# One stationary operand for the high and low gate weights of an mLSTM, and a first weight word in two transfers

## The chip, the cores and the metric

The kernel runs on one core of a Trainium2 chip. Five engines with instruction queues of their own take part: TensorE (PE, matmuls), VectorE (DVE), ScalarE (ACT), GpSimd (POOL) and SyncE (SP, which here only issues transfers). The metric is the device time of one execution in microseconds (us), as a median over runs.

## The reference

A trunk of two layers over 256 tokens of width 1024; the feed-forward width is 2816. All of it is computed in float32.

```
for l in range(2):
    x = layer_norm(ALPHA * x + 0.5 * swiglu(x, ffn_w_in[l, 0], ffn_w_out[l, 0]), ...)
    y = mlstm_mixer(x, ...) if l == 0 else window_attention(x, ...)
    x = layer_norm(ALPHA * x + y, ...)
    x = layer_norm(ALPHA * x + 0.5 * swiglu(x, ffn_w_in[l, 1], ffn_w_out[l, 1]), ...)

# swiglu: (silu(x @ w_gate) * (x @ w_up)) @ w_out
# mlstm_mixer, 4 heads, both directions:
p = x @ w_in                      # q, k, v, o, and 16 columns of gates
gates = p[..., 3072:] + gate_b    # input and forget gate, for each direction and head
logf = log_sigmoid(f_pre); g = cumsum(logf)
# weights exp(g_t - g_s + ig_s - m_t) between tokens, where m is a running maximum
# h = (weights * (q @ k)) @ v / max(|sum|, exp(-m)); both directions are added
# window_attention: 16 query heads, 4 key heads, |t - s| <= 128, a slope on the distance,
# a sink for each head in the softmax's denominator
```

## The kernel before

**High and low parts.** PE's fast float format (fp32r) keeps fewer bits than float32. So every operand is split in two: `hi`, the value rounded to fp32r, and `lo`, what is left. A product of two float32 matrices becomes three matmuls into the same accumulator, `hi*hi`, `hi*lo` and `lo*hi` (`mm3`). A weight word is a block of 128 x 1024 values (512 KB): SP brings it to a tile `raw`, ACT casts it to `w_hi`, DVE subtracts to get `w_lo` (`word`, `split`). The activations are kept transposed as `xT_hi` and `xT_lo`: PE turns a 128x128 block against the identity (`ident`), ACT or DVE casts the result, DVE subtracts. In the feed-forward parts sums of blocks (`S1` to `S4`, and `b` among the weights) let seven block products do the work of eight (`seven`).

**Order.** The kernel's functions don't issue instructions; they record them in a `Book`, from which all are emitted at the end. That is why every row of the profile bears one line, L472. PE's order is the order of the code. `cost` gives each step a planned duration, `latest` works back from PE's line to a due time of each step, and `sequence` lets each of DVE, ACT, POOL and SP take the step with the earliest due time among those that are ready in the plan. So a changed figure in `cost` moves all due times ahead of it, and with them the order on four engines.

**Start.** SP's first transfers are half of the first 128 tokens of x (256 KB), the first weight word (512 KB), half of the other tokens, and the next word. PE turns the identity 8 times, then x's first four blocks, then the identity 14 times more (`warm(14)`), whose results are not used. The first word is cast in two halves on ACT and DVE, each of which waits for the whole transfer. Then come the first products, `pw<-w_hi,xT_hi`.

**Gates.** The 16 gate columns lie in two tiles of 128 x 8 x 128 with zeros between them, `gw_hi` and `gw_lo`: input gates in output rows 0 to 63, forget gates in rows 64 to 127, the two directions 32 rows apart. For each of 8 blocks of the width `mm3` multiplies them with `xT`, 24 matmuls of 256 columns in all, into `pg`. DVE and ACT make the logarithm of the sigmoid and the sums and maxima along the tokens from it (tiles `scan` and `ig`), and PE turns the result later (`pw<-ident,ig`).

**Attention.** At its setup POOL builds the table of distances (`fwd`, `back`, `dist`) and takes a step of the layer norm (`rs`). Then for each of 8 pairs of heads: PE makes scores (`pw<-kT,q`); DVE adds slope and distance and takes the maximum (`ISA` in the order of instructions, CUSTOM_DVE in the profile, to `sc` and `nse`); ACT takes the exponential and sums it (`ACTIVATE sc,nse`); DVE adds the sink's part and takes the reciprocal (`nse`); POOL scales `sc` by it; PE turns the four tiles (`pw<-ident,sc`); ACT and DVE split the result (`pr0`, `pr1`); PE multiplies with the values (`pw<-pr,v`). PE fills the time between with products for later heads and of the output (`py<-w_hi,q_hi`).

Of the kernel before, what the change touches and what calls it, by code (L numbers as in the profile page):

```python
# [170 lines left out]
class Book:  # L171


    def __init__(self, nc, pools):
        self.nc, self.pools = nc, pools
        self.steps, self.rooms = [], {kind: [] for kind in HOMES}
        self.tensor, self.vector, self.scalar = Queue(self, "PE"), Queue(self, "DVE"), Queue(self, "ACT")
        self.gpsimd, self.sync = Queue(self, "POOL"), Queue(self, "SP")
        self.loaded, self.table_users = None, []

# [67 lines left out]
    def cost(self, s):  # L248
# [3 lines left out]
        if s.engine == "PE":  # L252
            n = size(s.outs[0])
            s.takes, s.later = (109.0 if s.name == "transpose" else n / 2.4 + 13.3), 200.0
            if s.name == "matmul" and s.args[1].shape[0] == 64:
                s.takes = 111.0
        elif s.name == "dma_start":
# [218 lines left out]
def trunk_kernel(ctx: ExitStack, tc: tile.TileContext, x, ffn_w_in, ffn_w_out, ln_g, ln_b, ml_w_in, ml_gate_b,  # L476
# [21 lines left out]
    def pair(p, *idx):  # L498
        return p[0][idx], p[1][idx]
# [36 lines left out]
    def two(w, r0, c0):  # L536
        return w[r0:r0 + 256, c0:c0 + 512].rearrange("(k p) f -> p k f", p=128)

    def wide(w, r0, c0, **kw):
        return split(word(two(w, r0, c0), 2), **kw)  # L540

# [169 lines left out]
    def ffn(l, i, n, pending, last):  # L711
# [28 lines left out]
        if start:  # L740
            gu(0)
            load_x(1, 0)
            warm(14)

# [227 lines left out]
    def mlstm(l, n, pending, last):  # L972
        va = [both(f"v{t}", (128, 4, 272), "tall") for t in range(2)]
        gwi = both("gw", (128, 8, 128))
        for p in gwi:
            nc.gpsimd.memset(p.bitcast(F32), 0.0)
        for g in range(4):
            c = 64 * (g % 2) + 32 * (g // 2)
            split_evac(pair(gwi, A, A, slice(c, c + 4)), gw[:, :, 4 * g:4 * g + 4])
        for t in range(2):  # L980
# [34 lines left out]
        nc.vector.tensor_scalar(fa, fe, 1.0, None, op0=OP.add)  # L1015
        nc.vector.scalar_tensor_tensor(fa, fa, 1.0, fe, op0=OP.subtract, op1=OP.subtract)
        nc.vector.tensor_sub(fl, fa, fl)
        nc.vector.tensor_add(fm, fm, fl)
        cum = fl
        u = ig  # L1020
        for d in range(2):
            q = slice(32 * d, 32 * d + 32)
            ord_ = slice(None, None, -1) if d else A
            nc.vector.tensor_tensor_scan(cum[q, ord_], ones[q].to_broadcast([32, S]), fm[q, ord_], 0.0, op0=OP.mult, op1=OP.add)
        nc.vector.tensor_sub(u, ig, cum)
        pm = fm
        for d in range(2):
# [3 lines left out]
        for d in range(2):  # L1031
            nc.gpsimd.dma_start(most[0:128:32, d], pm[32 * d:32 * d + 4])
        ex = fe
        nc.vector.scalar_tensor_tensor(ex, cum, -1.0, pm, op0=OP.mult, op1=OP.subtract)
# [19 lines left out]
        def weights(h):  # L1054
# [3 lines left out]
            for d, blk in ((0, 1), (1, 0)):  # L1058
                c = 32 * d + h
# [53 lines left out]
        def divide(h):  # L1113
            den, ys = part.pop(h)
            nc.vector.tensor_max(den, den, ecol[:, :, h:64:32])
            nc.vector.reciprocal(den, den)
# [294 lines left out]
```

## Time and profile before

| | |
|---|---|
| median of 3 runs | 913.88 us (913.88 to 913.98) |
| the profiled execution | 913.72 us, its span 911.8 us |
| mean granted clock of PE | 0.997 |
| PE busy | 902.6 us, 4459 matmuls |
| DVE busy | 811.4 us |
| ACT busy | 584.2 us |
| POOL busy | 145.4 us |
| moved by transfers | 208.53 MB |

The span is the time between the first and the last instruction of the profiled execution; what lies around it (1.9 us) belongs to the execution's time. A row of the timeline gives the start in us from the span's start, the busy time of the row's instructions in us, the engine, the line, the operation with its tiles (written tile, arrow, read tiles), the sizes and the number of instructions that the row joins; in brackets the idle time of the engine before it, and what it waited for. Matmuls overlap in their pipeline: the busy time of a row is longer than the step from one matmul to the next.

### The profile page before, as it was taken

The page shows a single profiled execution, that of the slowest core. Times are in us where ns is not written, and L with a number is a line of the kernel's source. Part 1 is how long each engine was busy: PE and PEld are TensorE (multiplying, and loading weights), DVE is VectorE, ACT ScalarE, POOL GpSimd, SP SyncE. Part 2 cuts the span into 40 slices and gives each one's busy share as a digit, 9 for nine tenths or more (in the row PEclk, how much of TensorE's full clock was granted, in tenths as well). Part 3 has the DMA queues.
Part 4 walks back from the last instruction along what each step waited for, and adds up shares of the span by engine and source line. Part 5 has one row for each costly group of instructions (what it writes and reads, how often), then busy time and mean ns, then how long its engine had stood idle before and what let it go on. Part 6 is the DMA issues. An engine that isn't in the chain of part 4 may idle for free.

```text
span 911.8 us, 12602 instructions
## 1 busy us (share of the span) xinstructions
PE 902.6 (99%) x4459; PEld 757.3 (83%) x4459; DVE 811.4 (89%) x985; ACT 584.2 (64%) x793; POOL 145.4 (16%) x177
## 2 busy tenths in 40 slices
PE   9999999999999999999999999999999999999996
PEld 7888888889988888888888888888898888888885
DVE  7989999887798989999889899998998698999976
ACT  7676777548554667776646667775488555677760
POOL 0112111206011011111011121211513202111100
PEclk9999999999999999999999999999999999999998
DMA  9999998844494688988965989989452367999831
GB/s 329 388 311 218 299 307 231 282 151 142 137 309 149 198 200 252 289 262 241 364 224 167 240 204 317 278 240 336 142 162 94 131 213 152 260 282 236 293 70 47
DMA packets 100703, 208.53 MB, mean 229 GB/s; under 512 B 6904, under 2 KB 21264, under 8 KB 100640
## 3 DMA queue, kind: packets, MB, share of 16 engines
q1 hardware_dynamic: 82944, 174.09, 54.6%
q0 software_dynamic: 17696, 33.65, 21.4%
q8 instruction: 35, 0.57, 0.3%
q14 instruction: 28, 0.23, 0.1%
HBM read 206.65 MB, written 1.05 MB: 228 GB/s over the span
## 4 chain that ended last, share of the span: by engine, by line
PE 93%; DVE 3%; ACT 1%; issue 1%; POOL 0%; DMA 0%; DVEq 0%; POOLq 0%
PE pw L472 60%; PE py L472 33%; DVE w_lo L472 1%; DVE x L472 1%; ACT sc L472 1%; DVE pr L472 0%; DMA x<-in_x_dram 0%; DVE stats L472 0%; ACT pr L472 0%; ACT w_hi L472 0%; POOL sc L472 0%; DVE xT_lo L472 0%; DVE sc L472 0%; DVE few L472 0%; POOL rs L472 0%
## 5 line engine op out<-in xcount | busy, mean ns | idle before, releaser
L472 ACT CAST w_hi<-b 128x1024 fp32r<-128x1024 f32 x224 | 234.1, 1055 | 88.8 <-PE py L472 44.1
L472 DVE TENSOR_TENSOR w_lo<-b,w_hi 128x1024 fp32r<-128x1024 f32 x224 | 267.0, 1218 | 17.5 <-ACT w_hi L472 17.1
L472 ACT CAST w_hi<-raw 128x1024 fp32r<-128x1024 f32 (+1 forms) x181 | 186.8, 1047 | 97.9 <-PE py L472 63.5
L472 DVE TENSOR_TENSOR w_lo<-raw,w_hi 128x1024 fp32r<-128x1024 f32 (+1 forms) x181 | 218.2, 1224 | 21.3 <-ACT w_hi L472 19.7
L472 PE MATMUL pw<-w_hi,xT_hi 128*128 128x512 f32 x480 | 189.5, 396 | 0.0
L472 PE MATMUL pw<-w_hi,xT_lo 128*128 128x512 f32 x480 | 187.1, 391 | 0.1
L472 PE MATMUL pw<-w_lo,xT_hi 128*128 128x512 f32 x480 | 186.2, 390 | 0.0
L472 PE MATMUL pw<-w_hi,S 128*128 128x512 f32 x512 | 162.8, 389 | 0.0
L472 POOL DMA_DIRECT2D b<-in_ffn_w_in_dram x64 | 77.4, 1211 | 470.3 <-DVE b L472 272.5
L472 PE MATMUL py<-w_hi,h_hi 128*128 128x512 f32 x317 | 125.2, 395 | 0.0
L472 PE MATMUL py<-w_hi,h_lo 128*128 128x512 f32 x317 | 123.6, 390 | 0.0
L472 PE MATMUL py<-w_lo,h_hi 128*128 128x512 f32 x317 | 123.5, 389 | 0.0
L472 PEld LDWEIGHTS pw<-w_hi,S 128*128 128x128 f32 x512 | 96.1, 188 | 19.9
L472 PEld LDWEIGHTS pw<-w_hi,xT_lo 128*128 128x128 f32 x480 | 90.0, 188 | 20.2 <-DVE xT_lo L472 0.9
L472 PEld LDWEIGHTS pw<-w_lo,xT_hi 128*128 128x128 f32 x480 | 90.3, 188 | 17.8
L472 PEld LDWEIGHTS pw<-w_hi,xT_hi 128*128 128x128 f32 x480 | 90.0, 188 | 17.4 <-ACT xT_hi L472 0.2
L472 PE MATMUL pw<-w_lo,S 128*128 128x512 f32 x256 | 99.6, 389 | 0.0
L472 DVE TENSOR_TENSOR b<-b,b 128x1024 f32<-128x1024 f32 x64 | 78.1, 1221 | 1.2
L472 PEld LDWEIGHTS py<-w_hi,h_lo 128*128 128x128 f32 x317 | 59.5, 188 | 12.6
L472 PEld LDWEIGHTS py<-w_lo,h_hi 128*128 128x128 f32 x317 | 59.6, 188 | 11.9
L472 PEld LDWEIGHTS py<-w_hi,h_hi 128*128 128x128 f32 x317 | 59.6, 188 | 11.7
L472 PEld LDWEIGHTS pw<-w_lo,S 128*128 128x128 f32 x256 | 48.0, 188 | 10.0
(198 smaller groups left out, 1079.0 us busy)
## 6 DMA issues: line engine op xcount, KB each, us to landing
b<-in_ffn_w_in_dram SPq DMA_DIRECT2D x128, 512.0 KB, 7.0
raw<-in_ffn_w_out_dram SPq DMA_DIRECT2D x88, 512.0 KB, 7.4
b<-in_ffn_w_in_dram POOLq DMA_DIRECT2D x64, 512.0 KB, 8.6
raw<-in_ffn_w_in_dram SPq DMA_DIRECT2D x32, 512.0 KB, 7.3
raw<-in_ml_w_in_dram SPq DMA_DIRECT2D x24, 512.0 KB, 9.2
raw<-in_ffn_w_in_dram SPq DMA_DIRECT2D x32, 256.0 KB, 6.6
raw<-in_at_w_in_dram SPq DMA_DIRECT2D x12, 512.0 KB, 8.5
raw<-in_ml_w_out_dram SPq DMA_DIRECT2D x8, 512.0 KB, 4.6
```

Of the source, the lines that this page charges most:

```text
L472: getattr(engines[s.engine], s.name)(*[real(x) for x in s.args], **{k: real(x) for k, x in s.kw.items()})
```

## The change

Three edits, and the new orders that follow from the third.

1. The gates' high parts stand in columns 0 to 63 and their low parts in columns 64 to 127 of one stationary tile `gwi`. For each of the 8 blocks it is multiplied with `xT_hi` and `xT_lo`: 16 matmuls. The products with the low part come out in rows 64 to 127 of `pg`; ACT copies these rows to `gl`, and the additions that bring in the bias on DVE add `gl` too. (`lo*lo`, which was left out before, is now part of the sum.) Both directions share the forget gate's steps of 32 rows. One memset on POOL goes.
2. The first word comes in two transfers of 128 x 512 values (`halves`), each with its own cast and subtraction, and `warm(14)` becomes `warm(4)`.
3. `cost` plans a matmul with 64 rows of contraction with 58.5 ns for 111, and adds 88 ns wherever PE goes from such matmuls to others or back.

```
         if s.engine == "PE":
             n = size(s.outs[0])
             s.takes, s.later = (109.0 if s.name == "transpose" else n / 2.4 + 13.3), 200.0
-            if s.name == "matmul" and s.args[1].shape[0] == 64:
-                s.takes = 111.0
+            narrow = s.name == "matmul" and s.args[1].shape[0] == 64
+            if narrow:
+                s.takes = 58.5
+            if narrow != self.narrow:
+                s.takes, self.narrow = s.takes + 88.0, narrow
...
-    def wide(w, r0, c0, **kw):
-        return split(word(two(w, r0, c0), 2), **kw)
+    def wide(w, r0, c0, halves=False):
+        src = two(w, r0, c0)
+        return split(word([src[:, k:k + 1] for k in range(2)] if halves else src, 2), halves=halves)
...
-            r = 64 * (g % 2) + 32 * (g // 2)
+            r = 32 * (g % 2) + 4 * (g // 2)
             nc.gpsimd.dma_start(gbias[r:r + 4], ml_gate_b[0, 4 * g:4 * g + 4].rearrange("(p o) -> p o", o=1))
...
-            warm(14)
+            warm(4)
...
-        gwi = both("gw", (128, 8, 128))
-        for p in gwi:
-            nc.gpsimd.memset(p.bitcast(F32), 0.0)
+        gwi = nc.tile("gw", (128, 8, 128), "big", FR)
+        nc.gpsimd.memset(gwi.bitcast(F32), 0.0)
         for g in range(4):
-            c = 64 * (g % 2) + 32 * (g // 2)
-            split_evac(pair(gwi, A, A, slice(c, c + 4)), gw[:, :, 4 * g:4 * g + 4])
+            c = 32 * (g % 2) + 4 * (g // 2)
+            split_evac((gwi[:, :, c:c + 4], gwi[:, :, 64 + c:68 + c]), gw[:, :, 4 * g:4 * g + 4])
...
         for k in range(8):
-            mm3(pg, pair(gwi, A, k), pair(xT, A, k), k == 0, k == 7)
+            for f in range(2):
+                nc.tensor.matmul(pg, gwi[:, k], xT[f][:, k], start=k == f == 0, stop=k == 7 and f == 1)
         scan = nc.tile("scan", (128, 4, S), "big")
         fa, fe, fl, fm = [scan[0:64, n_] for n_ in range(4)]
-        ig = temp("ig", S)[0:64]
-        nc.vector.tensor_scalar(fa, pg[64:128], gbias[64:128], None, op0=OP.add)
-        nc.vector.tensor_scalar(fm, pg[64:128], gbias[64:128], 0.0, op0=OP.add, op1=OP.min)
-        nc.vector.tensor_scalar(ig, pg[0:64], gbias[0:64], None, op0=OP.add)
-        nc.vector.scalar_tensor_tensor(fa, fm, 2.0, fa, op0=OP.mult, op1=OP.subtract)
-        nc.scalar.activation(fe, fa, AF.Exp)
-        nc.scalar.activation(fl, fe, AF.Ln, bias=1.0)
+        gl, ig = temp("gl", S)[0:64], temp("ig", S)[0:64]
+        nc.scalar.copy(gl, pg[64:128])
+        r, f_ = slice(0, 32), slice(32, 64)
+        nc.vector.scalar_tensor_tensor(fa[r], pg[f_], gbias[f_], gl[f_], op0=OP.add, op1=OP.add)
+        nc.vector.tensor_scalar(fm[r], fa[r], 0.0, None, op0=OP.min)
+        nc.vector.scalar_tensor_tensor(fa[r], fm[r], 2.0, fa[r], op0=OP.mult, op1=OP.subtract)
+        nc.scalar.activation(fe[r], fa[r], AF.Exp)
+        nc.scalar.activation(fl[r], fe[r], AF.Ln, bias=1.0)
+        for d in range(2):
+            nc.vector.scalar_tensor_tensor(ig[32 * d:32 * d + 32], pg[r], gbias[r], gl[r], op0=OP.add, op1=OP.add)
...
```

The lines left out keep the steps of the scans, with 32 rows where both directions share them and 36 in place of 32 between the directions' results.

The orders: ACT at the start of the program, before. Names end in the number of the buffer; `raw_79`, `raw_91` and `raw_98` are the first three words, `py` the turned blocks of x, `S3` a sum of two of them.

```order
L472 CAST w_hi_118<-raw_79 128x512 x2
L472 CAST xT_hi_71<-py_133 128x4x128
L472 CAST w_hi_145<-raw_91 128x1024
L472 COPY x10_153<-py_133 128x512
L472 CAST xT_hi_71<-py_161 128x4x128
L472 CAST w_hi_176<-raw_98 128x1024
L472 CAST xT_hi_71<-py_166 128x4x128
L472 CAST S3_190<-S3_169 128x512
L472 CAST w_hi_197<-raw_108 128x1024
```

The same place now; the first three words are `raw_79`, `raw_93` and `raw_106`.

```order
L475 CAST w_hi_109<-raw_79 128x512 x2
L475 CAST xT_hi_71<-py_123 128x4x128
L475 COPY x10_134<-py_123 128x512
L475 CAST w_hi_142<-raw_93 128x1024
L475 CAST S3_150<-S3_145 128x512
L475 CAST xT_hi_71<-py_154 128x4x128
L475 CAST xT_hi_71<-py_161 128x4x128
L475 CAST w_hi_174<-raw_106 128x1024
L475 CAST S1_183<-S1_169 128x512
```

The third word's cast now stands behind the cast of S3 and both casts of x; it stood ahead of S3 and of the second of them.

DVE in attention, heads 0 and 1, before: `nse_6262` belongs to head 0, `sc_6318` and `nse_6319` to head 1, each a pair of heads.

```order
L472 ISA nse_6262 128x1
L472 TENSOR_TENSOR nse_6262<-nse_6262 128x4
L472 RECIPROCAL nse_6262<-nse_6262 128x4
L472 SCALAR_TENSOR_TENSOR q1_lo_6244<-py_6234,qs_col_6051,q1_hi_6238 128x256
L472 ISA sc_6318,nse_6319<-pw_6288,dist_6027,few_74 128x256
L472 ISA nse_6319 128x1
```

The same place now, where `nse_6246` belongs to head 0, `sc_6292` and `nse_6293` to head 1.

```order
L475 ISA nse_6246 128x1
L475 ISA sc_6292,nse_6293<-pw_6272,dist_5993,few_74 128x256
L475 ISA nse_6293 128x1
L475 TENSOR_TENSOR nse_6246<-nse_6246 128x4
L475 RECIPROCAL nse_6246<-nse_6246 128x4
```

The first score step of head 1 moved ahead of head 0's sum and reciprocal, for which POOL's scaling waits. The same happens between heads 1 and 2 and between heads 4 and 5.

ACT at the end of attention, before: `pr0_6795` and `pr1_6809` are head 5's, `sc_6815`, `sc_6830` and `nse_6816` head 7's, `pr0_6859` and `pr1_6864` head 6's.

```order
L472 CAST pr0_6795<-pw_6767 128x512
L472 CAST pr1_6809<-pw_6797 128x512
L472 ACTIVATE sc_6815,nse_6816<-sc_6815,nse_6816 128x256
L472 ACTIVATE sc_6830,nse_6816<-sc_6830,nse_6816 128x256
L472 ACTIVATE sc_6815,nse_6816<-sc_6815,nse_6816 128x256
L472 ACTIVATE sc_6830,nse_6816<-sc_6830,nse_6816 128x256
L472 ACTIVATE nse_6816<-nse_6816,few_74 128x2
L472 CAST pr0_6859<-pw_6849 128x512
L472 CAST pr1_6864<-pw_6854 128x512
L472 ACTIVATE nse_6816<-nse_6816,few_74 128x2
L472 CAST q1_hi_6238<-pw_6822 128x256
L472 ACT_TABLE_LOAD
```

The same place now, where `pr0_6778` and `pr1_6820` are head 5's, `pr0_6850` and `pr1_6858` head 6's.

```order
L475 CAST pr0_6778<-pw_6754 128x512
L475 ACTIVATE sc_6787,nse_6788<-sc_6787,nse_6788 128x256
L475 ACTIVATE sc_6803,nse_6788<-sc_6803,nse_6788 128x256
L475 ACTIVATE sc_6787,nse_6788<-sc_6787,nse_6788 128x256
L475 CAST pr1_6820<-pw_6785 128x512
L475 ACTIVATE sc_6803,nse_6788<-sc_6803,nse_6788 128x256
L475 ACTIVATE nse_6788<-nse_6788,few_74 128x2 x2
L475 ACT_TABLE_LOAD
L475 CAST q1_hi_6222<-pw_6811 128x256
L475 CAST pr0_6850<-pw_6840 128x512
L475 CAST pr1_6858<-pw_6847 128x512
```

Head 5's second cast moved behind three of head 7's exponentials, and head 7's sums and the table load moved ahead of head 6's casts. On POOL at attention's setup two of the selects for `fwd` and `back` moved ahead of the step on `rs`; PE's order is the same as before but for the gates and the ten turns.

More of the change, by code (lines that the diff above doesn't have):

```diff
@@ L178, in __init__ @@
         self.gpsimd, self.sync = Queue(self, "POOL"), Queue(self, "SP")
-        self.loaded, self.table_users = None, []
+        self.loaded, self.table_users, self.narrow = None, [], False
     def tile(self, name, shape, kind, dtype=F32):
@@ L1004, in mlstm @@
         for k in range(8):
-            mm3(pg, pair(gwi, A, k), pair(xT, A, k), k == 0, k == 7)
+            for f in range(2):
+                nc.tensor.matmul(pg, gwi[:, k], xT[f][:, k], start=k == f == 0, stop=k == 7 and f == 1)
         scan = nc.tile("scan", (128, 4, S), "big")
         fa, fe, fl, fm = [scan[0:64, n_] for n_ in range(4)]
-        ig = temp("ig", S)[0:64]
-        nc.vector.tensor_scalar(fa, pg[64:128], gbias[64:128], None, op0=OP.add)
-        nc.vector.tensor_scalar(fm, pg[64:128], gbias[64:128], 0.0, op0=OP.add, op1=OP.min)
-        nc.vector.tensor_scalar(ig, pg[0:64], gbias[0:64], None, op0=OP.add)
-        nc.vector.scalar_tensor_tensor(fa, fm, 2.0, fa, op0=OP.mult, op1=OP.subtract)
-        nc.scalar.activation(fe, fa, AF.Exp)
-        nc.scalar.activation(fl, fe, AF.Ln, bias=1.0)
[L1015 to L1019, printed above, removed]
+        gl, ig = temp("gl", S)[0:64], temp("ig", S)[0:64]
[8 more added lines that the diff above has]
+            nc.vector.scalar_tensor_tensor(ig[32 * d:32 * d + 32], pg[r], gbias[r], gl[r], op0=OP.add, op1=OP.add)
+        nc.vector.tensor_scalar(fa[r], fe[r], 1.0, None, op0=OP.add)
+        nc.vector.scalar_tensor_tensor(fa[r], fa[r], 1.0, fe[r], op0=OP.subtract, op1=OP.subtract)
+        nc.vector.tensor_sub(fl[r], fa[r], fl[r])
+        nc.vector.tensor_add(fm[r], fm[r], fl[r])
+        cum = fe
         u = ig
@@ L1023, in mlstm @@
             ord_ = slice(None, None, -1) if d else A
-            nc.vector.tensor_tensor_scan(cum[q, ord_], ones[q].to_broadcast([32, S]), fm[q, ord_], 0.0, op0=OP.mult, op1=OP.add)
+            nc.vector.tensor_tensor_scan(cum[q, ord_], ones[r].to_broadcast([32, S]), fm[r, ord_], 0.0, op0=OP.mult, op1=OP.add)
         nc.vector.tensor_sub(u, ig, cum)
-        pm = fm
+        pm = fl
         for d in range(2):
@@ L1031, in mlstm @@
         for d in range(2):
-            nc.gpsimd.dma_start(most[0:128:32, d], pm[32 * d:32 * d + 4])
-        ex = fe
+            nc.gpsimd.dma_start(most[0:128:32, d], pm[36 * d:36 * d + 4])
+        ex = cum
         nc.vector.scalar_tensor_tensor(ex, cum, -1.0, pm, op0=OP.mult, op1=OP.subtract)
@@ L1058, in weights @@
             for d, blk in ((0, 1), (1, 0)):
-                c = 32 * d + h
+                c = 36 * d + h
                 nc.scalar.activation(w[:, d, 2], w[:, d, blk], AF.Exp, bias=ucol[:, 1 - blk, c:c + 1], scale=-1.0)
@@ L1114, in divide @@
             den, ys = part.pop(h)
-            nc.vector.tensor_max(den, den, ecol[:, :, h:64:32])
+            nc.vector.tensor_max(den, den, ecol[:, :, h:64:36])
             nc.vector.reciprocal(den, den)
```

## The prediction

> **What bounds the kernel now.** I read the busy line first, then the chain of work that ended last, then the waits of PE alone.
>
> ```profile
> PE 902.6 (99%) x4459; PEld 757.3 (83%) x4459; DVE 811.4 (89%) x985; ACT 584.2 (64%) x793; POOL 145.4 (16%) x177
> PE 93%; DVE 3%; ACT 1%; issue 1%; POOL 0%; DMA 0%; DVEq 0%; POOLq 0%
> ```
> ```profile
> PE py L472 <- DVE ident L472: 1.7, 1, 1.7
> ```
> PE is busy for 902.6 of 911.8 us, it makes 93% of the chain, and the list of its waits holds one entry, the wait for the identity at the start. So an edit counts for what it takes from PE's instructions or from the short gaps between them, and DVE at 89% is the engine that can open new gaps. The list leaves short gaps out; they are read below from the starts of successive matmuls.
>
> **The start (first word in two transfers, 4 turns for 14).** The timeline of the first 14 us, PE, then ACT, then DVE: start, busy time, engine, operation, and in brackets the idle time before it with what ended it.
>
> ```profile
> 1.71 1.97 PE L472 MATMUL py<-ident 128*128 128x128 f32 x8 [1.71 <-DVE ident L472]
> 3.77 1.11 PE L472 MATMUL py<-ident,x 128*128 128x128 f32 x4
> 4.67 2.31 PE L472 MATMUL py<-ident 128*128 128x128 f32 x14
> 6.74 0.71 PE L472 MATMUL pw<-w_hi,xT_hi 128*128 128x512 f32 x2
> 7.29 0.60 PE L472 MATMUL py<-ident,x 128*128 128x128 f32 x4
> 13.89 0.39 PE L472 MATMUL pw<-w_lo,xT_hi 128*128 128x512 f32 x1
> ```
> ```profile
> 5.74 0.91 PE L472 MATMUL py<-ident 128*128 128x128 f32 x6
> ```
> ```profile
> 5.58 1.14 ACT L472 CAST w_hi<-raw 128x512 fp32r<-128x512 f32 x2 [3.50 <-DMA raw<-in_ffn_w_in_dram]
> 10.69 0.59 ACT L472 CAST xT_hi<-py 128x512 fp32r<-128x512 f32 x1 [0.59 <-PE py L472]
> 11.23 1.05 ACT L472 CAST w_hi<-raw 128x1024 fp32r<-128x1024 f32 x1
> ```
> ```profile
> 4.92 0.69 DVE L472 CAST xT_hi<-py 128x512 fp32r<-128x512 f32 x1 [3.26 <-PE py L472]
> 6.25 1.28 DVE L472 TENSOR_TENSOR w_lo<-raw,w_hi 128x512 fp32r<-128x512 f32 x2
> 12.32 1.23 DVE L472 TENSOR_TENSOR w_lo<-raw,w_hi 128x1024 fp32r<-128x1024 f32 x1 [0.25 <-ACT w_hi L472]
> ```
> The ten turns that go ran from 4.67 to 6.98, while ACT waited for the word and cast it (5.58 + 1.14 = 6.72). They filled waiting, so taking them out gains nothing by itself; what can gain is the word. The first x (256 KB) was there at 3.77 and the word (512 KB) at 5.58, so I put its first half at their middle, 4.7 (an estimate), and its cast at 0.57 (half of 1.14) later. The first product then waits for the high part of x on DVE, 4.92 + 0.69 = 5.61, and starts at about 5.7 instead of 6.74; the second waits for the second half, which lands no earlier than the whole did: 5.58 + 0.57 = 6.15. Behind them stand four turns of the second x, the next transfer in SP's queue. At the word's rate (0.9 per 256 KB) it lands at 6.5; the split puts one more issue ahead of it, for which no row has a price, so I take 6.9, which is 0.4 before the 7.29 of now.
>
> That lead doesn't last. On ACT the third word's high half now stands behind the sum S3 and both casts of x. The last four of the second pair of turns would end near 10.7, the cast of x behind them (0.59) at 11.4, the word's high half (1.05) at 12.45 and its low half on DVE (1.23) at 13.7. Before, the low half was ready at 12.32 + 1.23 = 13.55 for a product at 13.89, so a product 0.35 earlier (13.54) has to wait for it until about 13.8. I take -0.1, nearest to what this chain allows. The bounds are -0.45 (the lead stays whole, when ACT gets through sooner) and +0.2 (the third word 0.3 later still).
>
> At the start the chip's clock matters too: four turns took 1.11 us at 3.77 and 0.60 at 7.29, and the six from 5.74 (0.91) hold one last wide step, so the pace doubled near 5.9, when PE had run nothing but turns, 4.2 us after the first. I count the switch at the same time after the change, since its 16 turns start at the same moments. The Trainium skill, "TensorE: Matmul & The Clock Gate", Part 4: PE-mode transpose, has it that transposes don't count as busy work and that with them the full rate "doesn't engage"; then the switch would come only with the products. These rows disagree, for the pace doubled before any product ran; by the row the term is 0, by the rule it is the rival B below.
>
> **The gates.** The timeline of PE, DVE and ACT there:
>
> ```profile
> 194.88 0.28 PE L472 MATMUL pw<-xT_hi,gw_hi 128*128 128x256 f32 x1
> ...
> 197.63 0.28 PE L472 MATMUL pw<-xT_hi,gw_lo 128*128 128x256 f32 x1
> ```
> ```profile
> 197.96 0.89 DVE L472 TENSOR_SCALAR scan<-pw,few 64x256 f32<-64x256 f32 x2 [1.57 <-PE pw L472]
> ...
> 204.87 0.42 DVE L472 SCALAR_TENSOR_TENSOR scan<-scan 64x256 f32<-64x256 f32 x1
> ```
> ```profile
> 199.39 0.87 ACT L472 ACTIVATE scan<-scan 64x256 f32<-64x256 f32 x2 [3.72 <-DVE scan L472]
> ```
> ```profile
> 208.75 0.34 PE L472 MATMUL pw<-ident,ig 64*128 64x64 f32 x2
> ```
> The first of the 24 matmuls starts at 194.88, the last at 197.63: 2.75 / 23 = 0.1196 each. Eight go: -0.96, all on PE, which is the bound there. Nothing was idle for the operands before them, so I take it whole; its bounds are -0.96 and 0 (if the chain behind becomes late). That chain of scans ends at 204.87 + 0.42 = 205.29 and PE turns its result at 208.75, a cover of 3.46. Added to it are a copy of 64 rows on ACT (at most 0.44, an Exp of the same size being half of 0.87), one more addition on DVE (at most 0.45, half of 0.89), one word's cast now ahead of the Exp on ACT (1.05) and one word's subtraction inside the chain on DVE (1.23): 3.17 in all, still under 3.46. The end of the gates' matmuls comes 0.96 earlier, and so do the turns, so the two move together. The missing memset on POOL frees POOL, which has no part in the path here. If the cover went, PE would wait at 208.75 by what exceeds it.
>
> **Setup of attention.** Only the planner's order changes here: POOL does two of its selects for the distance table in the 5.43 us in which it had waited for `rs`.
>
> ```profile
> 644.75 1.53 POOL L472 TENSOR_TENSOR rs<-rs,few 128x1 f32<-128x1 f32 x1 [5.43 <-DVE rs L472]
> ...
> 650.67 2.13 POOL L472 TENSOR_TENSOR dist<-fwd,back 128x512 f32<-128x512 f32 x1
> ```
> ```profile
> 645.78 1.22 DVE L472 TENSOR_TENSOR w_lo<-raw,w_hi 128x1024 fp32r<-128x1024 f32 x1
> ...
> 651.92 1.97 DVE L472 TENSOR_TENSOR w_lo<-raw,w_hi 128x1024 fp32r<-128x1024 f32 x1
> 653.81 1.27 DVE L472 TENSOR_TENSOR xT_lo<-py,xT_hi 128x512 fp32r<-128x512 f32 x2
> ```
> ```profile
> 653.82 0.39 PE L472 MATMUL pw<-w_hi,xT_hi 128*128 128x512 f32 x1
> 654.05 0.39 PE L472 MATMUL pw<-w_lo,xT_hi 128*128 128x512 f32 x1
> 654.54 0.50 PE L472 MATMUL pw<-w_hi,xT_lo 128*128 128x512 f32 x1
> 654.88 0.40 PE L472 MATMUL pw<-w_hi,xT_hi 128*128 128x512 f32 x1
> ```
> The steps of 0.49 and 0.34 between these products, against the 0.23 of the first step, are 0.38 of waiting for the low part of x. DVE came to it late because its subtraction took 1.97 beside POOL's `dist` and 1.22 without. The table now ends some 3 us earlier, so most of this goes: I take -0.3, with bounds 0 and -0.38.
>
> **Heads 0 and 1 of attention.** On DVE the first score step of head 1 comes ahead of head 0's sums.
>
> ```profile
> 674.52 0.28 PE L472 MATMUL pw<-kT_hi,q_lo 64*128 64x256 f32 x2
> ...
> 677.35 0.60 PE L472 MATMUL pw<-ident,sc 128*128 128x128 f32 x4
> ```
> ```profile
> 674.59 0.16 DVE L472 TENSOR_TENSOR nse<-nse 128x4 f32<-128x4 f32 x1 [1.30 <-ACT nse L472]
> ...
> 675.35 0.47 DVE L472 CUSTOM_DVE_ANT_0 sc<-pw,dist,few 128x256 f32<-128x256 f32 x1
> ```
> ```profile
> 675.17 1.84 POOL L472 TENSOR_SCALAR sc<-sc,nse 128x256 f32<-128x256 f32 x4 [19.07 <-DVE nse L472]
> ```
> The score step can't start before its products end, near 674.9, and takes 0.47. The sums slip from 674.59 to 675.38, and POOL's four scalings, now done at 677.01, end at about 677.8. PE turns the fourth scaled tile at 677.35 + 3 x 0.109 = 677.67: a wait of 0.2. Head 1 goes the same way by less, 0.1. Together +0.3; bounds 0 (another step slips in there) and +0.8 (the whole delay of 0.79).
>
> **Tail of attention.** ACT's order changes: for head 5 the second half's cast stands behind three exponentials; head 7's sums come sooner.
>
> ```profile
> 707.77 1.62 PE L472 MATMUL pw<-pr,v 128*128 128x256 f32 x12
> 709.92 1.03 PE L472 MATMUL pw<-ident,sc 128*128 128x128 f32 x8
> 711.48 1.82 PE L472 MATMUL pw<-pr,v 128*128 128x256 f32 x12
> 713.84 1.92 PE L472 MATMUL pw<-ident,sc 128*128 128x128 f32 x8
> ```
> The last eight turns take 1.92 against 1.03, so 0.89 waits for head 7's scaled tiles on POOL, and the last values 1.82 against 1.62, 0.20 more. Both should go: -1.09. Against that the values of head 5 now wait for their late cast, by about two exponentials, which I take at half of 0.87 each, and a small step, some +1.0. The load of ACT's table moves ahead of head 6's casts, but PE needs those only after head 7's turns and it is just covered. Sum -0.1; bounds -1.1 (no new wait) and +1.0 (the new wait comes, the old ones stay).
>
> **Sum.** -0.1 - 0.96 - 0.3 + 0.3 - 0.1 = -1.16 against the profiled execution, 913.72 us (0.16 under the median of 913.88; its span is 911.8). That makes 912.6 in a profiled execution and 912.7 as a median.
>
> **The rivals.**
>
> A, clearly faster. ACT gets to the third word in time (start -0.45), the waits of the setup all go (-0.38), heads 0 and 1 find POOL in time (0), and the tail loses both its waits without the new one (-1.07). With -0.96 that is -2.86: 911.0. For it: every new wait above is between 0.2 and 1.0 us on an engine with idle time close by (POOL's 19.07 before its scaling, ACT at 64%). Against it: three estimates must all fall to one side.
>
> B, no change. The half pace lasts longer. If PE's activity counts from the first product, 5.7, and takes the same 4.2, the clock is at half pace to 9.9. In these 4.2 us PE does 2.1 us of its work of now, where the forecast has it do 3.2 (12 products of 0.23 and four turns of 0.109); that costs 1.1, which cancels the rest: -1.16 + 1.1 = -0.06, 913.8. For it: ten turns less stand before the products. Against it: the pace doubled before any product ran. The skill's Part 4 rule, told above, is the reason for which one could expect it.
>
> C, slower. The same switch, but missed once: a gap after the 4 turns (from 5.3 to 5.7 PE now has nothing to do) makes the clock fall back for a second period, to about 13.9 or 14. It costs 1.1 + 0.5 x 4.2 = 3.2, with the rest +2.0: 915.9. It decides when the half pace lasts past 13.7, where 3.0 of loss are reached (1.16 + 1.83). For it: the gap is new. Against it: in the trace PE also idles from 0 to 1.71 and the pace needed one period only.
> The Trainium skill, same page, Part 1: The HAM clock gate, describes the budget as some 3.4 us of busy time in a free-running window, so that it varies from run to run; the 4.2 of these rows includes that phase, and no run here shows it varying.
>
> **How the numbers follow.** The forecast has 0.55, A 0.29, B 0.08, C 0.08. A measurement of this kernel can tell about 0.2% from no change, 1.83 us: 912.05 and 915.71. The forecast and B lie inside, 0.63; A outside below, 0.29; C above, 0.08. The range runs from 911.2, near the end of A, to 914.3, which takes in B and the forecast's +1.0 and +0.5 ends; what it leaves out is C (0.08) and the outer part of A (about 0.12). The forecast's own range is 912.1 to 913.5.
>
> **What would show it.** Right: 16 matmuls of the gates at 0.12 each and their result turned with no new gap; first product near 5.7, the second x turned near 6.9, a short gap near 13.5; the pace of turns 0.109 from 5.9 on; no step over 0.23 among the products near 654; a turn of head 0 late by 0.2 near 676; the last eight turns of attention 1.03 long and a wait of about 1 in head 5's values. Wrong: a half pace of the clock beyond 6, a gap before the gates' result is turned, or new gaps in the feed-forward parts, whose order on ACT and DVE I take to be equal in effect.

## The result and the profile after

The change makes the kernel slower by about a tenth of a per cent: 915.07 us (914.74 to 916.64, 20 runs) against 913.93 (913.47 to 914.64, 20 runs beside them), a ratio of 1.0014 with a 95% interval from 1.0008 to 1.0021. The forecast was 912.7, in a range from 911.2 to 914.3. The profiled execution of the changed kernel took 914.74 us, its span 912.9; that of before took 913.72 with a span of 911.8.

The busy line of the changed kernel, and the list of PE's waits:

```profile
PE 900.8 (99%) x4441; PEld 755.1 (83%) x4441; DVE 813.5 (89%) x986; ACT 585.3 (64%) x794; POOL 145.3 (16%) x176
```
```profile
PE py L475 <- DVE ident L475: 1.7, 1, 1.7
PE pw L475 <- POOL sc L475: 0.9, 1, 0.9
PE pw L475 <- DVE w_lo L475: 0.6, 1, 0.6
PE pw L475 <- ACT pr L475: 0.6, 1, 0.6
PE py L475 <- DMA x<-in_x_dram: 0.6, 1, 0.6
```
PE does 1.8 us less work, yet the span grows by 1.1. Before, the list held the first entry alone; four waits are new. To see what each is worth I laid the starts of the same matmuls in the two traces side by side; what counts is where their distance changes:

| place | forecast | traces |
|---|---|---|
| start, up to 15 us | -0.1 (-0.45 to +0.2) | +0.98 |
| gates | -0.96 | -0.99 |
| attention's setup | -0.3 (-0.38 to 0) | -0.33 |
| heads 0 and 1 | +0.3 (0 to +0.8) | +1.04 |
| attention's tail | -0.1 (-1.1 to +1.0) | +0.02 |
| all on PE | -1.16 | +0.72 |
| behind PE's last matmul | none | +0.42 |

The last row is the rest of the span, and the forecast has no term for it. From PE's last matmul to the end it takes 7.00 us before and 7.42 now. In both traces the last output is issued 4.05 us behind that matmul and lands about 2.0 us after its issue; from its landing to the end it takes 0.92 before and 1.35 now. There SP waits for the completion signals of its transfers, eight in a fixed order, and one that has already come takes it about 0.06 us. Before, the last output's signal is the last of the eight, and the others are done with while that output is under way. With one transfer more in the program it is the first, and seven more follow it: 7 x 0.06 = 0.42. SP's waits for the output, before and now:

```profile
SPq L1407 <- DMA out_dram<-x: 1.2, 2, 0.6
```
```profile
SPq L1414 <- DMA out_dram<-x: 1.6, 1, 1.6
```
All eleven traces of this study with the first word in two transfers have 7.41 to 7.43 us behind PE's last matmul, all six with one transfer 6.99 or 7.00. So these 0.42 belong to the split, far from the place where it was made.

**The start.** ACT, DVE and PE of the changed kernel, from 9 to 15 us:

```profile
10.76 0.58 ACT L475 CAST xT_hi<-py 128x512 fp32r<-128x512 f32 x1
11.92 0.59 ACT L475 CAST xT_hi<-py 128x512 fp32r<-128x512 f32 x1 [0.57 <-DVE S L475]
12.40 1.05 ACT L475 CAST w_hi<-raw 128x1024 fp32r<-128x1024 f32 x1
```
```profile
8.81 0.69 DVE L475 TENSOR_TENSOR xT_lo<-py,xT_hi 128x512 fp32r<-128x512 f32 x1 [1.56 <-ACT x L475]
...
11.19 0.69 DVE L475 TENSOR_TENSOR S<-x,py 128x512 f32<-128x512 f32 x1
...
13.48 1.23 DVE L475 TENSOR_TENSOR w_lo<-raw,w_hi 128x1024 fp32r<-128x1024 f32 x1 [1.00 <-ACT w_hi L475]
```
```profile
13.74 0.39 PE L475 MATMUL pw<-w_hi,xT_hi 128*128 128x512 f32 x1
14.76 0.50 PE L475 MATMUL pw<-w_lo,xT_hi 128*128 128x512 f32 x1 [0.63 <-DVE w_lo L475]
```
The product with the third word's low half, at 13.89 before, starts at 14.76; PE loses 0.90 there. ACT's second cast of x stands ahead of that word's cast, as the orders show, but it also waits 0.57 us for DVE's `S`, which reads the same turned block `py`. Nothing in the program's data asks for that wait: both only read. In the same way the low part of x on DVE (8.81) waits for ACT's copy of its block, and PE loses another 0.30 near 9.6 us. Against these 1.2 stand 0.29 that PE was ahead when it began to turn the second x.

**Head 0.** DVE, POOL and PE of the changed kernel:

```profile
676.76 1.22 DVE L475 TENSOR_TENSOR w_lo<-raw,w_hi 128x1024 fp32r<-128x1024 f32 x1
```
```profile
676.83 1.49 POOL L475 TENSOR_SCALAR sc<-sc,nse 128x256 f32<-128x256 f32 x1
```
```profile
677.00 0.49 PE L475 MATMUL pw<-ident,sc 128*128 128x128 f32 x3
678.38 0.33 PE L475 MATMUL pw<-ident,sc 128*128 128x128 f32 x1 [0.89 <-POOL sc L475]
```
Four scalings took 1.84 before, 0.48 each. Now the fourth alone takes 1.49. It starts 0.07 after a subtraction on DVE and ends 0.35 after that one's end. Against before, the scaling starts 0.30 later and the subtraction 0.20 earlier: it was 0.43 ahead and is now 0.07 behind.

**Gates, setup and tail.** PE at the end of the gates and where their result is turned, and DVE's last step of the chain between:

```profile
197.63 0.28 PE L475 MATMUL pw<-xT_lo,gw 128*128 128x256 f32 x1
197.75 0.40 PE L475 MATMUL pw<-w_hi,xT_hi 128*128 128x512 f32 x1
...
208.78 0.34 PE L475 MATMUL pw<-ident,ig 64*128 64x64 f32 x2
```
```profile
206.75 0.42 DVE L475 SCALAR_TENSOR_TENSOR scan<-scan 64x256 f32<-64x256 f32 x1
```
The products behind the gates start at 197.75 as before, though PE came 0.98 late. The chain ends at 207.17, so 1.6 of the cover of 3.46 is left.

PE at attention's setup and in its tail:

```profile
654.10 0.39 PE L475 MATMUL pw<-w_lo,xT_hi 128*128 128x512 f32 x1
654.32 0.39 PE L475 MATMUL pw<-w_hi,xT_lo 128*128 128x512 f32 x1
654.55 0.39 PE L475 MATMUL pw<-w_hi,xT_hi 128*128 128x512 f32 x1
```
```profile
708.40 0.87 PE L475 MATMUL pw<-pr,v 128*128 128x256 f32 x6
709.89 1.23 PE L475 MATMUL pw<-pr,v 128*128 128x256 f32 x6 [0.62 <-ACT pr L475]
...
713.22 1.71 PE L475 MATMUL pw<-pr,v 128*128 128x256 f32 x12
...
715.46 1.03 PE L475 MATMUL pw<-ident,sc 128*128 128x128 f32 x8
```
At the setup the steps are even: POOL's `dist` now starts at 647.60, and DVE's subtraction behind it takes 1.21 in place of 1.97 (an earlier one meets `dist` now and takes 2.31, without a wait of PE). In the tail the values of head 5 wait, and the last eight turns take 1.03 in place of 1.92.

### The profile page after: what moved, and what is told of

It is laid out like the page before. It is cut to its first block, busy times and chain, and to the rows that moved or that the text cites. A ratio compares the mean times of both kernels' runs of the same rounds, so it can differ in the third digit from the quotient of the medians.

```text
span 912.9 us, 12569 instructions
## 1 busy us (share of the span) xinstructions
PE 900.8 (99%) x4441; PEld 755.1 (83%) x4441; DVE 813.5 (89%) x986; ACT 585.3 (64%) x794; POOL 145.3 (16%) x176
## 3 DMA queue, kind: packets, MB, share of 16 engines
HBM read 206.65 MB, written 1.05 MB: 228 GB/s over the span
## 4 chain that ended last, share of the span: by engine, by line
PE 97%; DVE 1%; DMA 1%; ACT 0%; POOL 0%; issue 0%; SPq 0%; DVEq 0%; POOLq 0%
PE pw L475 62%; PE py L475 34%; DMA x<-in_x_dram 1%; DVE x L475 0%; POOL sc L475 0%; DVE w_lo L475 0%; DVE few L475 0%; DVE sc L475 0%; DVE S L475 0%; SPq L475 0%; ACT xT_hi L475 0%; ACT sc L475 0%; ACT w_hi L475 0%; DVEq L1414 0%; DVE pr L475 0%
```

## The experiments

Fifteen kernels, each timed in eleven runs beside runs of the kernel before on the same chip, whose median in these four groups (a to d) was 914.1 to 914.3. Beside the changed kernel it was 913.93, so a difference between medians of different groups is uncertain by some 0.3 us; the changed kernel lies 1.14 above before in its own group. The last column is where in the profiled execution PE's half pace ended (steps of 0.43 between products and 0.213 between turns, 0.23 and 0.109 after it; a step in between holds the end, which is read off to about 0.1).

| kernel | median | runs | ratio to before, 95% | half pace to |
|---|---|---|---|---|
| a1 gates alone | 913.39 | 912.56 to 913.90 | 0.9990 (0.9981 to 0.9998) | 7.9 |
| a2 split word, 14 turns | 915.78 | 915.18 to 916.87 | 1.0021 (1.0012 to 1.0030) | 7.3 |
| a3 4 turns alone | 913.54 | 913.10 to 915.86 | 0.9998 (0.9989 to 1.0007) | 8.1 |
| a4 costs alone | 915.13 | 914.58 to 915.77 | 1.0010 (1.0002 to 1.0019) | 6.2 |
| b1 S1 behind | 914.94 | 914.11 to 916.58 | 1.0008 (1.0000 to 1.0017) | 5.5 |
| b2 start's orders | 914.38 | 913.64 to 916.43 | 1.0008 (0.9999 to 1.0017) | 11.7 |
| b3 subtraction moved | 915.53 | 914.22 to 917.47 | 1.0015 (1.0007 to 1.0024) | 5.5 to 7.2 |
| b4 tail | 915.14 | 914.71 to 916.50 | 1.0011 (1.0002 to 1.0020) | 10.1 |
| c1 head 0 | 914.18 | 913.89 to 915.97 | 1.0004 (0.9996 to 1.0013) | 11.0 |
| c2 split word, 4 turns | 915.45 | 915.09 to 917.54 | 1.0018 (1.0009 to 1.0027) | 8.0 |
| c3 gates, 4 turns | 914.23 | 912.27 to 915.62 | 0.9998 (0.9989 to 1.0007) | 10.6 |
| c4 start and head 0 | 913.35 | 912.98 to 914.44 | 0.9992 (0.9983 to 1.0001) | 9.6 |
| d1 changed, 14 turns | 916.31 | 915.89 to 916.80 | 1.0023 (1.0014 to 1.0032) | 7.4 |
| d2 c4 with 14 turns | 914.06 | 913.46 to 914.48 | 0.9998 (0.9989 to 1.0006) | 7.8 |
| d3 gates, costs, head 0 | 913.09 | 912.24 to 914.00 | 0.9986 (0.9978 to 0.9995) | 5.0 |

**One part alone.** a1 is the kernel before with the gates' lines of the diff; a4 with the lines in `cost`. a2 takes the lines in `wide` and keeps `warm(14)`; a3 is before with

```
-            warm(14)
+            warm(4)
```

> The kernel before with the gates' edit alone (one stationary tile, 16 matmuls, the additions behind them); first word, turns and planned costs as before. Theory: the eight matmuls are worth 0.99 us on PE, as the comparison of the two traces shows at 195 to 198 us, and nothing later gives it back: 913.9 - 1.0 = 912.9, with PE ahead by 0.99 from 198 us to the end. Rival: the longer chain behind the gates costs a gap before their result is turned near 208 us and eats the gain: 913.9.

> The kernel before with the first word in two transfers, but all 14 turns kept. Theory: the 0.98 us lost at the start comes from the order on DVE and ACT that the plan makes of the extra transfer (the sum S1 ahead of the cast of the same block, the third word's cast behind both), so it appears here as well, near 14 us: 913.9 + 1.0 = 914.9. Rival: the loss comes from the missing turns (clock, or PE idle ahead of the first product), and with 14 turns the split costs nothing or gains 0.3: 913.6 to 913.9.

> The kernel before with 4 turns for 14 alone; the first word in one transfer. Theory: the turns filled waiting, and the clock's pace doubles near 5.9 us with 16 turns as with 26; the first product starts at 6.74 as before and the time stays at 913.9, within 0.3 (the plan shifts some steps of the feed-forward part by one place). Rival: with fewer turns the half pace lasts longer, the products up to 9.9 us take 0.45 us each in place of 0.23, and the time is 915.0.

> The kernel before with the planned costs of the narrow matmuls changed alone. Theory: attention's orders are those of the changed kernel, so PE gains 0.33 at the setup, loses 1.04 in head 0 and about 0 in the tail: +0.7, 914.6; mLSTM and start as before. Rival: head 0's loss needs the exact time at which the parts ahead deliver (POOL and DVE meet within 0.1 us), and with other arrival times it is gone: 913.9 - 0.3 = 913.6.

The gates give 0.7 on the median and 0.99 on PE, with no gap behind them: their theory holds. The costs alone cost 1.05 on the median, and their trace has head 0's loss (1.06) and the tail's even balance (+0.03), but only 0.1 of the setup's gain: there one of POOL's selects moves ahead of `rs`, not two. So head 0's loss is the planner's order, not a chance of arrival times. The split alone has the loss at the third word (0.90, at the products that lie at 13.7 to 14.2 us before), so it is the extra transfer and not the missing turns that brings the order in which S1 comes first. It also has the 0.30 at the low part of x and the 0.42 behind PE's last matmul; together these are 1.62 of its 1.7. Four turns alone agree with no change (a ratio of 0.9998; the median is 0.5 lower), but their runs spread over 2.8 us, and this was not expected.

**Orders moved by hand.** After the plan is made, single steps are put elsewhere in it:

```
         self.sequence()
+        for n, side, m in MOVES:
+            s = steps[n]
+            self.given.remove(s)
+            self.given.insert(self.given.index(steps[m]) + (side == "after"), s)
         return self.given
...
+MOVES = [(108, "after", 64), (109, "after", 108)]                                  # b1: S1, its cast
+MOVES = [(107, "after", 49), (128, "after", 50), (129, "after", 63),
+         (78, "before", 63), (108, "after", 64), (109, "after", 108)]              # b2: orders of before
+MOVES = [(5392, "after", 4935)]                                                    # b3: w_lo behind head 2's first score
+MOVES = [(5283, "before", 5287), (5284, "before", 5278), (5737, "after", 5278)]    # b4: pr1; its buffer changes too
+MOVES = [(4874, "after", 4855)]                                                    # c1: head 1's first score
```

> The changed kernel with one pair of steps moved at the start: DVE's sum S1 (from a turned block of x) goes behind the low parts that it preceded, and ACT's cast of S1 with it. Theory: ACT's cast of that block waited for S1 because both read the same accumulator bank; without that it follows the turns at 11.2 us in place of 11.92, the third word is ready 0.7 earlier and PE's gap near 14 us shrinks from 0.9 to 0.2: 915.1 - 0.7 = 914.4. Rival: the cast is late for ACT's order alone (the third word's cast behind both casts of x), S1 has no part in it: 915.1.

b1's ACT and PE:

```profile
10.82 1.08 ACT L482 CAST xT_hi<-py 128x512 fp32r<-128x512 f32 x2
11.79 2.26 ACT L482 CAST w_hi<-raw 128x1024 fp32r<-128x1024 f32 x2
```
```profile
14.16 0.50 PE L482 MATMUL pw<-w_lo,xT_hi 128*128 128x512 f32 x1
```
The two casts of x now stand in one row without a gap, the word's cast starts 0.61 sooner, and PE's wait shrinks by 0.69. ACT's order is otherwise the same, so the rival falls: S1 held the cast. The median follows only by 0.1 against the changed kernel's 915.07 (by 0.5 when each is set against before in its own group), and the intervals overlap, so this rests on the trace.

> The changed kernel with DVE's and ACT's orders at the start put back to those of before (S1, S3 and the copy of x behind, the third word's cast ahead of the second cast of x); two transfers and 4 turns stay. Theory: PE keeps the lead of 0.29 that the split gives at the second x, and the gap near 14 us goes: -1.27 against the changed kernel, 913.8. Rival: the lead is lost again to the third word, which is there no earlier than before: -0.98, 914.1.

b2's profile has the half pace up to 11.7 us, and in such an execution PE is too late for the third word to matter. The gap near 14 us is gone and the median is 0.7 lower (1.0 against before in its own group), less than the 1.27 of the theory, near the rival. The cleaner pair is d1 and d2 below, whose half pace ends at 7.4 and 7.8: with the orders of before at the start, d2 has neither the 0.90 nor the 0.30. The lead of 0.29 was no property of the kernel. It hangs on when the second x lands and on PE's pace: the turns of the second x start at 7.00 in the changed kernel's trace, and between 7.07 and 8.07 in the seven others with two transfers and 4 turns (7.29 before).

> The changed kernel with one step moved: the subtraction w_lo that starts on DVE at 676.76 us goes behind the first score step of head 2. The sums of head 0 stay as late as they are. Theory: head 0's fourth scaling on POOL takes 1.49 in place of 0.48 because it starts 0.08 us after that subtraction and the two can't run together; with the subtraction moved it takes 0.48, ends near 677.3, and PE's wait before the fourth turn falls from 1.05 to under 0.1: 915.1 - 1.0 = 914.1. Rival: the wait comes from the sums that are late by 0.65; the scaling stays as late as it is and the time does not change: 915.1.

b3's POOL, and PE's turns of head 0 and of head 1:

```profile
676.64 0.94 POOL L482 TENSOR_SCALAR sc<-sc,nse 128x256 f32<-128x256 f32 x2
```
```profile
677.25 0.71 PE L482 MATMUL pw<-ident,sc 128*128 128x128 f32 x4
...
682.80 1.05 PE L482 MATMUL pw<-ident,sc 128*128 128x128 f32 x4
```
The last two scalings take 0.94 together, the fourth 0.48, with the sums as late as in the changed kernel; PE's wait falls by 1.0. So late sums alone cost at most 0.1 (a turn row of 0.71, 0.60 before); it takes the subtraction beside the scaling. But in its new place it stands ahead of head 1's sums, and head 1 gives 0.73 back (a turn row of 1.05, 0.60 in the changed kernel); the median shows no gain.

> The changed kernel with the second cast of head 5 moved ahead of head 7's exponentials, its low part ahead of the last score step, in a buffer of its own (the plan had given it the buffer of the distance table, so it had to wait for the last score step; a prefetched weight block takes that buffer now, later). Theory: the values of head 5 no longer wait, and head 7's sums stay early: PE gains the 1.0 lost at 708.5 us: 915.1 - 0.9 = 914.2. Rival: head 7's sums become late in turn and the last eight turns wait 0.9 again: 915.1.

```profile
709.64 1.59 PE L486 MATMUL pw<-pr,v 128*128 128x256 f32 x12
...
714.12 1.95 PE L486 MATMUL pw<-pr,v 128*128 128x256 f32 x12 [0.62 <-ACT pr L486]
```
Head 5's values run through, a gain of 1.13, and head 6's wait in their place, 1.03 lost. Not the last turns, as the rival had it, but nearly the same result. In b4's trace the load of ACT's table (1.28 from 711.91) stands right ahead of head 6's casts (713.47); what would come of that load behind them, where it stood before, was not tried, so it is not shown that ACT's work bounds the tail in every order.

> The changed kernel with head 1's first score step put back behind head 0's sums, reciprocal and low part of q, as it was before. Theory: the sums come 0.4 earlier, POOL's fourth scaling starts ahead of the subtraction on DVE and takes 0.48, PE loses the wait of 1.05 and nothing else moves: 915.1 - 1.0 = 914.1. Rival: PE arrives earlier at head 1 and waits there for what the score steps gave it before, as when the subtraction was moved instead (0.75 given back): 914.8.

The fourth turn comes 1.06 earlier in c1's trace and nothing is given back; the median falls by 0.9 to 914.18. The theory holds. (Its profiled execution is one of the upper ones, 915.41, with the half pace up to 11.0.)

**The turns.** c2 has the lines in `wide` and `warm(4)`; c3 the gates' lines and `warm(4)`; c4 the changed kernel with the moves of b2 and c1. d1 is the changed kernel with `warm(14)`, d2 is c4 with it; d3 has the gates' and the costs' lines and c1's move, one transfer and 14 turns.

> The kernel before with the first word in two transfers and 4 turns, gates and planned costs as before. Theory: the third word's late low half costs 0.9 to 1.0, as with 14 turns, but where the clock's pace doubles late the ten turns no longer hold up the products, so it is less than the 1.7 of the split with 14 turns: 914.1 + 1.0 = 915.1. Rival: the number of turns has no part in it: 915.8, as with 14.

> The kernel before with the gates' edit and 4 turns for 14; the first word in one transfer and the planned costs as before. Theory: the gates bring 0.8 to 1.0 and the turns 0.2 to 0.5, and no gap is opened at the start or in attention: 914.1 - 1.2 = 912.9, better than both kernels. Rival: with fewer turns ahead of the products the clock's pace doubles later in most executions and takes the gates' gain back: 914.0.

> The changed kernel with both moves, the orders of before at the start and head 1's score step behind head 0's sums. Theory: the two losses are separate and large parts of both come back, 0.7 at the start and 1.0 in head 0: 915.1 - 1.7 = 913.4. Rival: at the start the time at which the clock's pace doubles decides, and the order there brings nothing on the median: 914.1.

c4 comes out as expected: 913.35, 1.7 below the changed kernel. c2 lies between theory and rival. c3 was expected to be the best and is not: its runs reach from 912.27, the second lowest of all, to 915.62. PE in c3's profile, then in a1's and d3's, whose turns are 14:

```profile
7.49 1.05 PE L472 MATMUL py<-ident,x 128*128 128x128 f32 x4
8.20 1.20 PE L472 MATMUL pw<-w_hi,xT_lo 128*128 128x512 f32 x2
9.20 1.05 PE L472 MATMUL pw<-w_lo,xT_hi 128*128 128x512 f32 x2
10.05 0.89 PE L472 MATMUL pw<-w_hi,xT_hi 128*128 128x512 f32 x2
10.77 0.62 PE L472 MATMUL pw<-w_lo,xT_hi 128*128 128x512 f32 x2
```
```profile
4.99 3.12 PE L472 MATMUL py<-ident 128*128 128x128 f32 x14
7.83 0.51 PE L472 MATMUL pw<-w_hi,xT_hi 128*128 128x512 f32 x1
```
```profile
4.72 1.84 PE L482 MATMUL py<-ident 128*128 128x128 f32 x14
6.33 0.91 PE L482 MATMUL pw<-w_hi,xT_hi 128*128 128x512 f32 x2
```
Two products take 1.05 at half pace and 0.62 at full. In c3 the half pace lasts into the products, to 10.6; 14 turns take 3.12 in a1, where it lasts to 7.9, and 1.84 in d3, where it ends at 5.0. Of the ten profiles with 4 turns five have it past 9 us, of the seven with 14 none past 8. The times go with it: of the ten, the three with an end by 7.2 lie 0.3 to 0.8 under their kernel's median, the five past 9 lie 0.0 to 1.8 above it.

> The changed kernel with its 14 turns back, the order at the start and in attention unchanged. Theory (the turns keep PE active, so that the clock's pace doubles before the products run): the runs lie within 1.5 us of each other, where the changed kernel's lay 1.9 apart, the half pace ends by 8 us, and the upper third of the times goes; the median stays at 915.0 or rises by up to 0.5, since the turns also hold the products up. Rival (the spread is chance and has nothing to do with the turns): the times spread over 2 us as before and the median is 915.1.

> The changed kernel with 14 turns, the orders of before at the start, and head 1's score step behind head 0's sums. Theory: no third word that comes late (-0.7 to -1.0), no late scaling (-1.05), a narrow spread: 913.3, at most 1.5 us wide. Rival: with 14 turns the products are held up and the split is worth nothing: 913.9.

> The gates' edit and the new planned costs, with head 1's score step behind head 0's sums; first word in one transfer and 14 turns, as before. Theory: the gates' 0.99 and a part of the setup's 0.33 stay, nothing is lost at the start, in head 0 or by the clock, and the tail is about even: 914.1 - 1.2 = 912.9, the best version, narrow like the kernel before. Rival: the tail's new order costs something once head 0 no longer waits (PE comes 1.05 earlier to head 5's values): 913.6.

d1's runs lie within 0.9 us, as the theory said, but its median is 1.2 higher, not 0.5: with 14 turns the changed kernel is narrow and slow. On the median 4 turns are lower than 14 in four pairs (d1 to the changed kernel -1.2, d2 to c4 -0.7, before to a3 -0.5, a2 to c2 -0.3) and higher in one (a1 to c3, +0.8). The intervals of the ratios overlap in every pair, so a gain is not shown; the wide spread is. Part of two of the pairs is the plan and not the clock: with 14 turns POOL has one select less ahead of `rs`, which costs d1 and d2 0.28 at the setup, and d2 has 0.28 of new gaps near 65 us that c4 does not have. The traces of c4 and d2 are even at 9.7 us. d2 stays above its theory; it lies 0.7 over a1. d3 is the best version, faster than both kernels: 913.09, 0.14% under before (interval 0.05% to 0.22%), with nothing lost in head 0.

## Why the prediction was wrong

It named the places on PE and got most of the sizes there. Gates (-0.96 for -0.99), setup (-0.3 for -0.33) and tail (-0.1 for +0.02, with the new wait of "some +1.0" at 1.13) hold. Two terms failed, by 1.1 and 0.7, and they make up nearly the whole distance on PE between -1.16 and +0.72. A third, the 0.42 behind PE's last matmul, is missing from the sum; with it PE's +0.72 becomes the 1.14 that the span and the median show.

**The start.** "The cast of x behind them (0.59) at 11.4, the word's high half (1.05) at 12.45 and its low half on DVE (1.23) at 13.7" is the right chain, and the word's casts and subtraction took what was said. The step that failed is the cast of x: it was taken to wait for PE's turns alone and started at 11.92, behind DVE's `S`. b1 showed it by moving `S`: 0.69 of the 0.90 came back. The low half came at 14.71, and the upper bound of +0.2 had no such wait in it. A wait of the same kind ate the lead at 9.6 us (0.30), where the low part of x on DVE came behind ACT's copy of the same block; with the copy moved back, in d2, it is gone.
The Trainium skill, "PSUM — Partial Sum Buffer", section "PSUM bank collisions raise a hardware error", says that two engines may not touch one bank at once within the same partitions, reads included, and that the compiler's scheduler adds a dependency between any two such instructions. These traces agree with the order that it forces: 0.57 us of ACT waiting for a reader on DVE, gone when the reader is moved. What the chip would do without the wait was not tried.

**Head 0.** "POOL's four scalings, now done at 677.01, end at about 677.8" took each of the four at the duration of before. The sums came later as forecast, and the subtraction on DVE came 0.20 sooner; so the fourth started 0.07 us behind it and took 1.49. The forecast had used just this meeting at the setup (1.97 against 1.22 for DVE beside POOL's `dist`) and did not look for it here. b3, which moves the subtraction, and c1, which moves the sums, show it from two sides.
The Trainium skill, "SBUF — State Buffer", section "SBUF: two separate sides", has a port pair which DVE and POOL share, held for a whole instruction by whichever starts first. The trace agrees: the fourth scaling began after DVE's 676.76 and could end only 0.35 after 677.98; before, it began ahead of the subtraction and took 0.47.

**The turns.** "Taking them out gains nothing by itself" and "I count the switch at the same time" both rested on one execution, in which the pace doubled at 5.9. Over seventeen profiles it doubles between 4.9 and 11.7 us. Rival B, no change because the half pace lasts longer, was a mechanism of this kernel after all, but of single executions: it goes with their spread, and on the median four turns show no clear loss or gain. In the changed kernel's profile the pace doubled at 4.9 (its last two turns start 0.17 apart, between 0.213 and 0.109), so this term has no part in its +0.98 at the start. That the end depends on how busy PE is ahead of the products fits the five of ten against none of seven; it was not shown by a direct test. A second source of spread stands beside it: with two transfers and 4 turns PE can wait for the second x, and b2's profiled execution, 1.8 over its median, lost 1.1 to the changed kernel's trace by that point and 1.6 more at half pace.

**Behind PE.** The sum ends with PE's last term, so it put the end of the program at nothing without a reason. One transfer more turned round the order in which SP finds its transfers done, for 0.42. It was not tried whether another number of transfers takes that back.

**What stays open.** The split costs 0.90, 0.30 and 0.42 in the traces, 1.62; a2 lies 1.7 above before and c2 1.35. With the orders put back (d2 against a1) the traces place 0.42 behind PE and 0.1 on PE (0.28 of new gaps near 65 us, most of it won back later); the medians have 0.7. What sets the end of the half pace, and how the spread divides between it and the landing of x, stays open.

## What to carry to other kernels

A step that is moved must be followed through what its engine shares: who else reads the same accumulator bank in the written order, and which instruction of DVE runs beside which of POOL. Here a shift of 0.5 us, from 0.43 ahead of a subtraction to 0.07 behind it, turned a scaling of 0.48 into one of 1.49.
A cost table that is nearer to the truth does not make a better order while the plan leaves such meetings out: here its correction cost 1.05 (a4), and one step moved by hand brought all of it back (d3 against a1).
One transfer more in a program can cost time at its end, so compare also what lies behind the last matmul.
One profile shows one phase of the clock at the start; before ten idle turns are called free, look at the start in several.

## What the runs showed of the hardware

PE's half pace ends at a different time in each execution, from 4.9 us (the changed kernel) to 11.7 (b2), 3.2 to 10.0 after the first turn. The Trainium skill, "TensorE: Matmul & The Clock Gate", Part 1: The HAM clock gate, calls the window free-running and the start run-variable; the traces agree in kind, and the 6.8 us between their ends are far more than the half microsecond either way that it gives for matmuls without a break; here PE also stood idle in between, and the ends with 14 turns, 5.0 to 7.9, lie closer. With 4 turns, between which and the products PE stands idle, the runs of one kernel lie up to 3.4 us apart (c3), against at most 1.8 with 14 (d3).

PE's first turn of x, which waits for the first 256 KB of x, starts at 3.48 to 4.14 us though their transfer is the first in every kernel. So even the start of the first real work on PE differs by 0.66 us from one execution to the next.
